# One pair of PSUM banks for two heads' scores in the attention mixers

## The chip, the cores and the metric

The kernel runs on one core of one Trainium2 chip. The metric is the device time of one execution in microseconds (us), as the median of repeated runs. The names of the engines in the rows are PE (matmul), PEld (weight load), DVE (VectorE), ACT (ScalarE), POOL (GpSimd) and SP (the engine that issues most transfers).

## The reference

Two layers of a diffusion backbone work on 256 context tokens and 256 latent tokens of width 1024. Each layer modulates its input with vectors computed from the conditioning, projects it, runs three groups of heads side by side (windowed attention A, a state space model B, differential attention C), projects their outputs and normalises. Layer 0 then runs a SwiGLU, layer 1 a mixture of 8 experts. Only the two attentions are touched by the change:

```python
# A: 6 query heads on 2 key heads of width 64, with a sink logit for each head
s = einsum(q, k) * 64 ** -0.5                  # latent: 512 keys, context: 256 keys
p = softmax(concat([s, sink]))                 # a band mask on the latent keys
y = einsum(p, v)

# C: 4 heads, each with two halves of width 32
s = einsum('bqhid,bkhid->bhiqk', q, k) * 32 ** -0.5
p = softmax(s)
a = p[:, :, 0] - lam * p[:, :, 1]
y = rmsnorm(einsum(a, v)) * (1 - lam_init)
```

## The kernel before, in words

Tokens lie in four tiles of 128 rows, two of context and two of latent tokens. Dense projections split each float operand in a high and a low half (`split`, L254 and L255) and make three matmuls of each (`mm3`, L268, L269 and L271). Weights come in through `load_w` (L246 to L249): a ring of four `raw` buffers, filled by transfers that SP issues in program order, so a buffer that is not given back holds up every later weight.

The function `mixers` of a layer starts several generators (dense projections, the three head groups, the output projection `op`, and `ada_group`, which computes modulation vectors for later from 64 tiny matmuls (L311) per group on weights `w_ada`) and `weave` takes their pieces in turn, by costs that each piece yields and by the weights in `PLAN`. A scheduler then fixes one order of instructions on each engine. Each engine runs its own list in that order and waits where an operand or a buffer is not there yet.

PSUM has eight banks of 128x512 floats. One pool shares them by tags: `S` three banks, `tp` two, `mm` two and `y` one. In the mixers `S` holds scores, `ada`, the token projections of the stage ahead (`TOKT`), the decayed products `p` (`T4`), `Sc` (`T5`) and `GT` (`T6`) of group B, and one of the two `xbc` projections.

An attention step is made of two heads. In `attn_A` (L865) a step is two key heads, whose score matmuls (L876) use 64 of the 128 rows of PE each; in `attn_C` (L901) it is the two halves of a head, with 32 rows each (L914). Each head has a bank of its own. `softmax` (L844) takes a maximum (L847), scales it (L849 or L851), and lets ACT write the exponentials `P` with their sum (L853). Group C then scales one half on ACT (L921), joins both with one product on DVE (L922), transposes the result (L860, copied by L862) and multiplies by the values (L927). Group A subtracts the sink, scales both heads (L890), transposes both and multiplies (L896). There are 42 steps: 14 with 256 keys, all in layer 0 (6 of A and 8 of C), and 28 with 512 keys (6 of A and 8 of C in each layer).

Of the kernel before, what the change touches and what calls it, by code (L numbers as in the profile page):

```python
# [12 lines left out]
F = mybir.dt.float32  # L13
# [3 lines left out]
AF = mybir.ActivationFunctionType  # L17
OP = mybir.AluOpType
AX = mybir.AxisListType.X
PSUM = bass.MemoryType.PSUM  # L20
# [5 lines left out]
LAT = (2, 3)  # L26
CTX = (0, 1)
# [17 lines left out]
CAPS, SLOTS = (64, 128, 128, 128, 128, 128, 64, 64), (0, 1, 6, 2, 7, 3, 4, 5)  # L45
NBUF = {"S": 3, "tp": 2, "mm": 2, "y": 1}
FDN = ("tp", "tp", "y", "mm"), ("S", "S", "S", "mm")
TOKT, TRA, ADA = "S", "tp", "S"
T1, T2, T3, T4, T5, T6, T7, T8, T9 = "y", "tp", "mm", "S", "S", "S", "mm", "tp", "tp"
OPT = 'mm'  # L50
HTD = 1
TL0 = CTX, LAT
# [58 lines left out]
def kernel(ctx: ExitStack, tc: tile.TileContext, I, out: bass.AP):  # L111
    nc = tc.nc
    V, S, G, T, SP = nc.vector, nc.scalar, nc.gpsimd, nc.tensor, nc.sync
# [4 lines left out]
    ps = ctx.enter_context(tc.tile_pool(name="ps", bufs=1, space=PSUM))  # L118
# [11 lines left out]
        return slice((t % 2) * 128, (t % 2) * 128 + 128)  # L130


    def p_(tag, name):
        return ps.tile([128, 512], F, name=name, tag=tag, bufs=NBUF[tag])

    def p_mm(name="mm"):
        return p_("mm", name)
# [68 lines left out]
    identb, maskF, maskB, ltb, onesb = (cb[:, i * 128:(i + 1) * 128] for i in range(5))  # L206
# [3 lines left out]
    def x_src(li, t):  # L210
        if li:
            return xscr[t * 128:(t + 1) * 128]
        return (I["ctx"] if t in CTX else I["x"])[0, (t % 2) * 128:(t % 2 + 1) * 128]


    def rstd_of(v, n, scale=1.0):
# [46 lines left out]
    def mm3(o, terms, start=True, stop=True):  # L263
# [6 lines left out]
        for i, (ah, al, bh, bl, wa) in enumerate(terms):  # L270
# [11 lines left out]
                    None, op0=OP.mult)  # L282
# [218 lines left out]
    def mixers(L, full_ctx, fill, tail):  # L501
# [5 lines left out]
        mp = att_ctx.enter_context(tc.tile_pool(name=f"att{li}", bufs=1, side="right"))  # L507
# [29 lines left out]
        def xbc_piece(f0, f1):  # L537
# [15 lines left out]

            if f0 == 0 and L.ready:

                pms = [p_mm("xbc"), p_("S", "xbc")]
                for ks in L.ready(sp, mp):
                    for k in ks:
                        for f in range(2):
                            mm(f, pms[f], 0, (k,))  # L560
                for f in range(2):
                    evac(f, pms[f], 0)
                    yield 5.1
                return
# [44 lines left out]
        def qTA(t):  # L609
            return yrow(t, 0, 3)  # L610

        def qTC(t):
            return yrow(t, 6, 8)
# [30 lines left out]

        def ktag(t):

            return "S" if t in CTX and not full_ctx else TOKT

        def use_C0(t, pm, a):
            V.tensor_tensor(dt[:, t], pm[:, 0:12], L.dtb, op=OP.add)  # L650
# [190 lines left out]
        def keys(t):  # L841
            return 256 if t in CTX else 512

        def softmax(po, n, nsink, sscale, st_, i):  # L844

            mx, nm, l = (st_[:, j, i:i + 1] for j in range(3))
            V.tensor_reduce(mx, po[:, :n], axis=AX, op=OP.max)  # L847
            if nsink is None:
                V.tensor_scalar(nm, mx, -sscale, None, op0=OP.mult)  # L849
            else:  # L850
                V.scalar_tensor_tensor(nm, mx, -sscale, nsink, op0=OP.mult, op1=OP.min)  # L851
            P = mp.tile([128, 512], F, name="P", tag="P", bufs=6)
            S.activation(P[:, :n], po[:, :n], AF.Exp, scale=sscale, bias=nm, accum_out=l)  # L853
            return P

        def transp(src, n):

# [7 lines left out]
        def attn_A(t):  # L865
            n = keys(t)
            nb = n // 128
            for g in range(3):
                st_ = sm.tile([128, 5, 2], F, name="smx", tag="smx", bufs=6)
                l, r, e = st_[:, 2], st_[:, 3], st_[:, 4]  # L870
                Ps, pos = [], []
                for kv in range(2):
                    po = p_("S", "SA")
                    pos.append(po)
                    b0 = 64 * kv
                    T.matmul(po[:, :n], qTA(t)[b0:b0 + 64, g], kTA[b0:b0 + 64, :n], start=True, stop=t in CTX)  # L876
                    if t == 2:
                        T.matmul(po[:, 384:512], identb, maskB, start=False, stop=True)
                    elif t == 3:
                        T.matmul(po[:, 256:384], identb, maskF, start=False, stop=True)  # L880
                for kv in range(2):
                    Ps.append(softmax(pos[kv], n, L.nsink[:, g, kv:kv + 1], 0.125, st_, kv))
                yield 0.0017 * n
                V.tensor_tensor(e, st_[:, 1], L.nsink[:, g], op=OP.subtract)
                S.activation(e, e, AF.Exp)
# [15 lines left out]
        def attn_C(t):  # L901
# [4 lines left out]
            for h in range(4):  # L906
                st_ = sm.tile([128, 5, 2], F, name="smx", tag="smx", bufs=6)
                l, r = st_[:, 2], st_[:, 3]
                Ps, pos = [], []
                for i in range(2):  # L910
                    po = p_("S", "SC")
                    pos.append(po)
                    b0 = 32 * ((2 * h + i) % 4)
                    T.matmul(po[:, :n], qTC(t)[b0:b0 + 32, h // 2], kTC[b0:b0 + 32, h // 2, :n], start=True,  # L914
                             stop=True)
                for i in range(2):
                    Ps.append(softmax(pos[i], n, None, 32 ** -0.5, st_, i))
                yield 0.0017 * n
                V.reciprocal(r, l)
                V.tensor_tensor(r[:, 1:2], r[:, 1:2], L.nlam, op=OP.mult)  # L920
# [796 lines left out]
                    yield v  # L1717

    mixers(L0, True, [ada_group(L0, 1), ada_group(L0, 2)], tail0())
    for _ in ada_group(L1, 0):  # L1720
        pass
    with tc.tile_pool(name="ffn", bufs=1) as fp:
# [2 lines left out]
    post.close()  # L1725


    for _ in layer_consts2(L1):
        pass

# [25 lines left out]
    mixers(L1, False, [ada_group(L1, 1), ada_group(L1, 2)], tail1())  # L1756
    tail_ctx.close()
    right.close()
    with ExitStack() as e:

        late = e.enter_context(tc.tile_pool(name="late", bufs=1))
        pools = [e.enter_context(tc.tile_pool(name=f"mraw{i}", bufs=1)) for i in range(3)]
        slots = [pools[i] for i, n in zip((1, 2, 0), MRB) for _ in range(n)]
        moe(L1, L1.pp, late, slots)
    post.close()


_INS = ["x", "c", "ctx", "c_ctx", "w_ada", "b_ada", "w_in", "attn_sink", "conv_w", "conv_b", "dt_bias", "a_log",
# [20 lines left out]
```

## Time and profile before

| what | value |
|---|---|
| median of 3 runs | 1867.69 us (1859.02 to 1873.53) |
| profiled execution | 1867.13 us, its span 1865.3 us |
| mean granted clock of PE | 0.96 of full speed |
| PE busy | 1712.7 us, 92% of the span |
| DVE, ACT, POOL busy | 1146.8, 873.3 and 327.9 us |

The profiled execution is one of the kernel before; 1.8 us of its time lie outside the span. The layer-0 mixers with their attention lie between some 60 and 400 us, the layer-1 mixers between some 850 and 1086 us. Between them stands the SwiGLU, behind them the experts.

### The profile page before, as it was taken

To read this page: it belongs to the slowest core of one execution; us is meant where nothing else is said; L and a number is where in the kernel's file an instruction comes from. 1 tells how busy PE (TensorE), PEld (TensorE's weight loads), DVE (VectorE), ACT (ScalarE), POOL (GpSimd) and SP (SyncE) were. 2 spreads that over 40 slices of the span, in tenths; PEclk is the share of its full clock that TensorE was granted. 3 is DMA by queue.
4 is the path that set the end of the run, shared out by engine and by line. 5 is a ranking of instruction groups with operands and counts; after the bars stand their busy time and mean duration, and the time that the engine had idled before them with its cause. 6 is when DMAs were issued, how large, how long until landed. Compare 5 with 4: busy or idle time off the path is not lost.

```text
span 1865.3 us, 26243 instructions
## 1 busy us (share of the span) xinstructions
PE 1712.7 (92%) x9355; PEld 1262.9 (68%) x9355; DVE 1146.8 (61%) x2242; ACT 873.3 (47%) x1460; POOL 327.9 (18%) x254
## 2 busy tenths in 40 slices
PE   5889999788999999979989949999999999999995
PEld 2677667576888888857866723486458537888884
DVE  4773577768433333485777670487068408898987
ACT  3533546437322233345435721375157317777774
POOL 1221023354310222952232420000000000000000
PEclk8999999798999999998999969999999999999998
DMA  9237254158432332546672359999999999999991
GB/s 309 79 105 229 81 173 150 46 173 257 125 102 89 93 101 90 164 154 216 200 228 72 109 183 397 409 406 401 369 409 406 380 396 408 408 370 359 340 324 50
DMA packets 251002, 436.37 MB, mean 234 GB/s; under 512 B 15056, under 2 KB 166232, under 8 KB 250864
## 3 DMA queue, kind: packets, MB, share of 16 engines
q1 hardware_dynamic: 248944, 429.81, 65.1%
q0 software_dynamic: 1920, 4.81, 0.9%
q8 instruction: 76, 1.25, 0.3%
q14 instruction: 62, 0.51, 0.1%
HBM read 431.34 MB, written 3.23 MB: 233 GB/s over the span
## 4 chain that ended last, share of the span: by engine, by line
PE 75%; DMA 8%; DVE 8%; issue 3%; ACT 2%; POOL 1%; SPq 0%; DVEq 0%; ACTq 0%; POOLq 0%
PE mg L1365 6%; PE mu L1365 5%; PE mdn L1365 5%; PE gu L271 4%; PE gu L268 4%; PE gu L269 4%; DMA raw<-in_w_ada 4%; PE mg L1519 3%; PE mg L1354 3%; PE mu L1519 3%; PE mu L1354 3%; PE mdn L1354 3%; DMA mraw<-in_exp_w_down 2%; PE tok L268 2%; PE tok L271 2%
## 5 line engine op out<-in xcount | busy, mean ns | idle before, releaser
L1345 DVE TENSOR_TENSOR mwl<-mraw,mwh 128x1024 fp32r<-128x1024 f32 (+2 forms) x372 | 388.7, 1103 | 26.1 <-ACT mwh L1344 18.3
L1344 ACT ACTIVATE mwh<-mraw 128x1024 fp32r<-128x1024 f32 (+2 forms) x372 | 339.8, 965 | 84.0 <-DMA mraw<-in_exp_w_gu 45.6
L255 POOL TENSOR_TENSOR wlo<-raw,whi 128x1024 fp32r<-128x1024 f32 (+2 forms) x93 | 230.7, 2487 | 480.5 <-ACT whi L254 422.2
L254 ACT ACTIVATE whi<-raw 128x1024 fp32r<-128x1024 f32 (+2 forms) x168 | 168.3, 1004 | 239.1 <-PE dn L269 71.9
L255 DVE TENSOR_TENSOR wlo<-raw,whi 128x1024 fp32r<-128x1024 f32 (+2 forms) x75 | 88.3, 1178 | 144.2 <-ACT whi L254 142.4
L268 PE MATMUL gu<-HI,whi 128*128 128x512 f32 (+1 forms) x400 | 144.4, 369 | 2.3 <-ACT whi L254 2.3
L269 PE MATMUL gu<-LO,whi 128*128 128x512 f32 (+1 forms) x400 | 144.9, 369 | 0.0
L311 PE MATMUL ada<-raw,cT 128*32 128x256 f32 x768 | 74.8, 429 | 41.8 <-DMA raw<-in_w_ada 38.3
L268 PE MATMUL tok<-whi,HI 128*128 128x256 f32 (+2 forms) x400 | 108.0, 299 | 4.4 <-ACT xin L545 3.1
L269 PE MATMUL tok<-whi,LO 128*128 128x256 f32 (+2 forms) x400 | 105.5, 293 | 5.3 <-DVE LO L439 4.1
L271 PE MATMUL gu<-HI,wlo 128*128 128x512 f32 (+1 forms) x400 | 98.5, 367 | 0.0
L268 PEld LDWEIGHTS tok<-whi,HI 128*128 128x128 f32 x400 | 78.6, 197 | 13.5 <-issue 4.4
L268 PEld LDWEIGHTS gu<-HI,whi 128*128 128x128 f32 x400 | 75.9, 191 | 15.8 <-ACT whi L254 2.5
L269 PEld LDWEIGHTS gu<-LO,whi 128*128 128x128 f32 x400 | 76.2, 191 | 12.7
L269 PEld LDWEIGHTS tok<-whi,LO 128*128 128x128 f32 x400 | 78.5, 197 | 9.2 <-DVE LO L439 5.9
L271 PEld LDWEIGHTS gu<-HI,wlo 128*128 128x128 f32 x400 | 70.3, 188 | 12.9
L268 PE MATMUL dn<-whi,ah 128*128 128x512 f32 x176 | 70.2, 399 | 4.9 <-ACT whi L254 4.9
L1354 PE MATMUL mdn<-mwl,mah 128*128 128x512 f32 x220 | 72.8, 399 | 0.9 <-DVE mwl L1345 0.5
L1365 PE MATMUL mdn<-mwh,mah 128*128 128x512 f32 x220 | 73.5, 399 | 0.0
L1528 DVE TENSOR_TENSOR msl<-msl,mu 128x512 f32<-128x512 f32 (+1 forms) x9 | 5.8, 643 | 110.0 <-PE mu L1519 110.0
L271 PE MATMUL tok<-wlo,HI 128*128 128x256 f32 (+2 forms) x400 | 71.4, 296 | 1.9 <-DVE nw L222 1.9
L1365 PE MATMUL mdn<-mwh,mal 128*128 128x512 f32 x220 | 72.5, 394 | 0.0
(358 smaller groups left out, 3645.6 us busy)
## 6 DMA issues: line engine op xcount, KB each, us to landing
mraw<-in_exp_w_gu SPq DMA_DIRECT2D x128, 1024.0 KB, 12.4
mraw<-in_exp_w_down SPq DMA_DIRECT2D x87, 1024.0 KB, 14.5
mraw<-in_exp_w_gu SPq DMA_DIRECT2D x64, 768.0 KB, 11.4
raw<-in_w_ada SPq DMA_DIRECT2D x88, 512.0 KB, 5.4
raw<-in_ffn_w_gu SPq DMA_DIRECT2D x100, 256.0 KB, 3.3
raw<-in_w_in SPq DMA_DIRECT2D x38, 512.0 KB, 5.1
raw<-in_ffn_w_down SPq DMA_DIRECT2D x30, 512.0 KB, 3.5
E<-cscr POOLq DMA_DIRECT2D x12, 384.0 KB, 7.1
```

The lines of the kernel that those rows point to most:

```text
L254: S.activation(hi, raw, AF.Copy)
L255: (eng or V).tensor_tensor(lo, raw, hi.bitcast(F), op=OP.subtract)
L268: T.matmul(o, ah, bh, start=start and i == 0, stop=False)
L269: T.matmul(o, *((ah, bl) if wa else (al, bh)), start=False, stop=False)
L271: T.matmul(o, *((al, bh) if wa else (ah, bl)), start=False, stop=stop and i == n - 1)
L311: T.matmul(pa[32 * j:32 * j + 32, hs], cT[:, k], w[j], start=(k == 0), stop=(k == KC - 1), tile_position=(0, 32 * j), skip_group_check=True)
L1344: S.activation(wh, raw, AF.Copy)
L1345: V.tensor_tensor(wl, raw, wh.bitcast(F), op=OP.subtract)
L1354: T.matmul(pc[:, :w], xh, wl[:, c * 512:c * 512 + w], start=False, stop=stop)
L1365: T.matmul(pc[:, :w], x, wh[:, c * 512:c * 512 + w], start=start and x is xh, stop=False)
L1519: T.matmul(p[hs, :n], Xf[:, kk, hs], raws[h][:, k, c * n:(c + 1) * n], start=kk == 0, stop=kk == KC - 1, skip_group_check=True)
L1528: V.tensor_tensor(sl[:, cs_], sl[:, cs_], p[:, :n], op=OP.mult)
```

## The change: one pair tile, one maximum, fewer banks for the others

In the mixers, `S` shrinks to one bank and a new tile `S2` of two adjacent banks, one buffer, takes the scores of both heads of a step. Both score matmuls are written one behind the other, the masks behind both. One reduction takes both maxima, one operation scales both, and ACT still writes two exponentials. What shared `S` before moves: the token projections, `p` and `GT` to `tp`, `Sc` and the second `xbc` to `mm`. In the dense stages `S` keeps three banks.

```diff
-TOKT, TRA, ADA = "S", "tp", "S"
-T1, T2, T3, T4, T5, T6, T7, T8, T9 = "y", "tp", "mm", "S", "S", "S", "mm", "tp", "tp"
+TOKT, TRA, ADA = "tp", "tp", "S"
+T1, T2, T3, T4, T5, T6, T7, T8, T9 = "y", "tp", "mm", "tp", "mm", "tp", "mm", "tp", "tp"
...
+    def stage(name):
+        if banks:
+            banks[0].close()
+        banks[:] = [ExitStack()]
+        banks.append(banks[0].enter_context(tc.tile_pool(name=name, bufs=1, space=PSUM)))
+        NBUF["S"] = 1 if name.startswith("mix") else 3
+
     def p_(tag, name):
-        return ps.tile([128, 512], F, name=name, tag=tag, bufs=NBUF[tag])
+        return (banks[1] if tag == "S" else ps).tile([128, 512], F, name=name, tag=tag, bufs=NBUF[tag])
+
+    def p_pair(name):
+        return banks[1].tile([128, 2, 512], F, name=name, tag="S2", bufs=1)
...
-                pms = [p_mm("xbc"), p_("S", "xbc")]
+                pms = [p_mm("xbc") for _ in range(2)]
...
-            return "S" if t in CTX and not full_ctx else TOKT
+            return "mm" if t in CTX and not full_ctx else TOKT
...
-        def softmax(po, n, nsink, sscale, st_, i):
-
-            mx, nm, l = (st_[:, j, i:i + 1] for j in range(3))
-            V.tensor_reduce(mx, po[:, :n], axis=AX, op=OP.max)
+        def softmax(po, n, nsink, sscale, st_):
+
+            mx, nm, l = (st_[:, j] for j in range(3))
+            V.tensor_reduce(mx, po[:, :, :n], axis=AX, op=OP.max)
...
-            P = mp.tile([128, 512], F, name="P", tag="P", bufs=6)
-            S.activation(P[:, :n], po[:, :n], AF.Exp, scale=sscale, bias=nm, accum_out=l)
-            return P
+            Ps = []
+            for i in range(2):
+                P = mp.tile([128, 512], F, name="P", tag="P", bufs=6)
+                S.activation(P[:, :n], po[:, i, :n], AF.Exp, scale=sscale, bias=nm[:, i:i + 1], accum_out=l[:, i:i + 1])
+                Ps.append(P)
+            return Ps
...
-                Ps, pos = [], []
+
+                po = p_pair("SA")
                 for kv in range(2):
-                    po = p_("S", "SA")
-                    pos.append(po)
-                    b0 = 64 * kv
-                    T.matmul(po[:, :n], qTA(t)[b0:b0 + 64, g], kTA[b0:b0 + 64, :n], start=True, stop=t in CTX)
...
-                for kv in range(2):
-                    Ps.append(softmax(pos[kv], n, L.nsink[:, g, kv:kv + 1], 0.125, st_, kv))
+                    bs = slice(64 * kv, 64 * kv + 64)
+                    T.matmul(po[:, kv, :n], qTA(t)[bs, g], kTA[bs, :n], start=True, stop=t in CTX)
+                if t in LAT:
+                    mask, ms_ = ((maskB, slice(384, 512)), (maskF, slice(256, 384)))[t - 2]
+                    for kv in range(2):
+                        T.matmul(po[:, kv, ms_], identb, mask, start=False, stop=True)
+                Ps = softmax(po, n, L.nsink[:, g], 0.125, st_)
...
-                Ps, pos = [], []
+                po = p_pair("SC")
                 for i in range(2):
-                    po = p_("S", "SC")
-                    pos.append(po)
-                    b0 = 32 * ((2 * h + i) % 4)
-                    T.matmul(po[:, :n], qTC(t)[b0:b0 + 32, h // 2], kTC[b0:b0 + 32, h // 2, :n], start=True,
-                             stop=True)
-                for i in range(2):
-                    Ps.append(softmax(pos[i], n, None, 32 ** -0.5, st_, i))
+                    bs = slice(32 * ((2 * h + i) % 4), 32 * ((2 * h + i) % 4) + 32)
+                    T.matmul(po[:, i, :n], qTC(t)[bs, h // 2], kTC[bs, h // 2, :n], start=True, stop=True)
+                Ps = softmax(po, n, None, 32 ** -0.5, st_)
...
+    stage("mix0")
...
     mixers(L0, True, [ada_group(L0, 1), ada_group(L0, 2)], tail0())
+    stage("dense0")
...
+    stage("mix1")
...
     mixers(L1, False, [ada_group(L1, 1), ada_group(L1, 2)], tail1())
...
+    stage("dense1")
```

In the orders below, `x2` behind a row means that it stands twice in a row, and the line numbers are those of each kernel: scores are L876 and L914 before, L893 and L928 after. On PE in layer 0, at the latent steps of group A, the two heads' scores (SA) stand apart before:

```order
L876 MATMUL SA<-kTA,YT 128x512
L878 LDWEIGHTS cb
L878 MATMUL SA<-cb 128x128
L896 MATMUL yA<-PT,vA 64x128 x4
L860 MATMUL PT<-cf,P 128x128 x2
L876 MATMUL SA<-kTA,YT 128x512
L878 LDWEIGHTS cb
L878 MATMUL SA<-cb 128x128
```

At the same place after, with the `ada` matmuls of the modulation behind the transposes:

```order
L893 MATMUL SA<-kTA,YT 128x512 x2
L897 LDWEIGHTS cb
L897 MATMUL SA<-cb 128x128
L897 LDWEIGHTS cb
L897 MATMUL SA<-cb 128x128
L912 MATMUL yA<-PT,vA 64x128 x4
L878 MATMUL PT<-cf,P 128x128 x4
L326 MATMUL ada<-raw,cT 32x256 x8
```

The scores of a step now follow each other, and so do its masks and its four transposes. On PE at the end of the layer-1 mixers, where the output projection (op) stands among the steps of group C, before:

```order
L271 MATMUL op<-wlo,HI 128x256 x2
L914 MATMUL SC<-kTC,YT 128x512
L860 MATMUL PT<-cf,P 128x128
L927 MATMUL yC<-vC,PT 128x64 x4
L860 MATMUL PT<-cf,P 128x128 x3
L914 MATMUL SC<-kTC,YT 128x512 x2
L268 MATMUL op<-whi,HI 128x256
L269 MATMUL op<-whi,LO 128x256
```

The last four steps of group C in that stage after:

```order
L928 MATMUL SC<-kTC,YT 128x512 x2
L286 MATMUL op<-wlo,HI 128x256
L939 MATMUL yC<-vC,PT 128x64 x4
L878 MATMUL PT<-cf,P 128x128 x4
L939 MATMUL yC<-vC,PT 128x64 x4
L928 MATMUL SC<-kTC,YT 128x512 x2
L878 MATMUL PT<-cf,P 128x128 x4
L939 MATMUL yC<-vC,PT 128x64 x4
L928 MATMUL SC<-kTC,YT 128x512 x2
L878 MATMUL PT<-cf,P 128x128 x4
L939 MATMUL yC<-vC,PT 128x64 x4
L928 MATMUL SC<-kTC,YT 128x512 x2
```

The rest of the output projection now stands ahead of these steps. On DVE in layer 1 before, maxima of later heads (L847) stand ahead of the product of an earlier step (L922):

```order
L847 TENSOR_REDUCE smx<-SC 128x1
L849 TENSOR_SCALAR smx<-smx 128x1
L847 TENSOR_REDUCE smx<-SC 128x1
L922 SCALAR_TENSOR_TENSOR P<-P,smx 128x512
L849 TENSOR_SCALAR smx<-smx 128x1
L919 RECIPROCAL smx<-smx 128x2
L847 TENSOR_REDUCE smx<-SC 128x1
L920 TENSOR_TENSOR smx<-smx,lcst 128x1
```

The same steps on DVE after, maximum (L862) and product (L934):

```order
L862 TENSOR_REDUCE smx<-SC 128x2
L864 TENSOR_SCALAR smx<-smx 128x2
L931 RECIPROCAL smx<-smx 128x2
L932 TENSOR_TENSOR smx<-smx,lcst 128x1
L934 SCALAR_TENSOR_TENSOR P<-P,smx 128x512
L942 TENSOR_TENSOR yC<-yC,lcst 128x64
L862 TENSOR_REDUCE smx<-SC 128x2
L864 TENSOR_SCALAR smx<-smx 128x2
```

Each step is now finished on DVE, up to its product, ahead of the maximum of the next.

## Rows read from the trace of the kernel before

**Rows 1.** Profile page, part 4: share of the ending chain by engine

```profile
PE 75%; DMA 8%; DVE 8%; issue 3%; ACT 2%; POOL 1%; SPq 0%; DVEq 0%; ACTq 0%; POOLq 0%
```

**Rows 2.** Windows: stretch, length; busy PE, PEld, DVE, ACT, POOL; granted clock, DMA share, GB/s

```profile
183.00:250.00 67.00, 67.00 (x493) 44.50 (x495) 43.91 (x141) 35.22 (x108) 4.75 (x2) 1.00 0.33 101
...
340.00:360.00 20.00, 14.25 (x58) 9.12 (x56) 13.28 (x51) 8.31 (x27) 9.30 (x7) 0.74 0.15 41
...
360.00:380.00 20.00, 14.57 (x60) 10.46 (x60) 12.29 (x53) 11.19 (x32) 2.05 (x3) 0.66 0.00 0
...
987.00:1054.00 67.00, 66.05 (x415) 44.36 (x415) 50.42 (x155) 43.73 (x107) 15.15 (x12) 0.97 0.30 93
...
1054.00:1072.00 18.00, 17.86 (x146) 16.73 (x145) 7.56 (x20) 9.91 (x25) 9.99 (x8) 1.00 0.15 54
```

**Rows 3.** Timeline of PE at scores: start, length (us), engine, line, operation, count

```profile
183.70 0.70 PE L876 MATMUL SA<-kTA,YT 64*128 64x256 f32 x4
...
197.12 0.70 PE L876 MATMUL SA<-kTA,YT 64*128 64x256 f32 x2
...
209.07 1.12 PE L876 MATMUL SA<-kTA,YT 64*128 64x512 f32 x2
210.13 0.44 PE L860 MATMUL PT<-cf,P 128*128 128x128 f32 x2
...
363.10 2.00 PE L914 MATMUL SC<-kTC,YT 32*128 32x512 f32 x2
...
1024.74 1.13 PE L914 MATMUL SC<-kTC,YT 32*128 32x512 f32 x4
...
1027.41 1.89 PE L914 MATMUL SC<-kTC,YT 32*128 32x512 f32 x4
...
1030.84 1.55 PE L914 MATMUL SC<-kTC,YT 32*128 32x512 f32 x4
...
1037.09 1.59 PE L914 MATMUL SC<-kTC,YT 32*128 32x512 f32 x4
```

**Rows 4.** Tile view of SA, the maxima: count, min/median/max (ns) of one

```profile
L847 DVE TENSOR_REDUCE smx<-SA x36: 414/684/692, 184.4 to 1017.3; 128x1 f32<-128x512 f32 x24, 128x1 f32<-128x256 f32 x12
```

**Rows 5.** Timeline of PE, DVE and ACT, parts of C steps in layer 1

```profile
1049.65 1.13 PE L914 MATMUL SC<-kTC,YT 32*128 32x512 f32 x4
...
1050.81 0.69 DVE L847 TENSOR_REDUCE smx<-SC 128x1 f32<-128x512 f32 x1 [0.73 <-PE SC L914]
...
1052.88 0.67 ACT L853 ACTIVATE P<-SC,smx 128x512 f32<-128x512 f32 x1
...
1054.95 0.75 DVE L922 SCALAR_TENSOR_TENSOR P<-P,smx 128x512 f32<-128x512 f32 x1 [0.92 <-ACT P L921]
...
1056.08 0.68 DVE L847 TENSOR_REDUCE smx<-SC 128x1 f32<-128x512 f32 x1
...
1057.09 0.68 ACT L853 ACTIVATE P<-SC,smx 128x512 f32<-128x512 f32 x1
```

**Rows 6.** Timeline of PE at the end of the layer-1 mixers

```profile
1063.02 0.28 PE L268 MATMUL op<-whi,HI 128*128 128x256 f32 x1
1063.14 0.28 PE L269 MATMUL op<-whi,LO 128*128 128x256 f32 x1
...
1071.28 1.10 PE L927 MATMUL yC<-vC,PT 128*128 128x64 f32 x8
```

**Rows 7.** Windows as in Rows 2, ahead of the layer-0 attention

```profile
120.00:130.00 10.00, 10.00 (x89) 7.71 (x87) 7.71 (x26) 3.70 (x11) 3.39 (x6) 1.00 0.02 4
130.00:140.00 10.00, 7.89 (x66) 6.38 (x58) 3.67 (x13) 1.31 (x3) 3.71 (x3) 1.00 0.95 276
```

**Rows 8.** Timeline of PE, the ada matmuls; in brackets a wait and its releaser

```profile
128.73 1.91 PE L311 MATMUL ada<-raw,cT 128*32 128x256 f32 x26
...
141.78 1.08 PE L311 MATMUL ada<-raw,cT 128*32 128x256 f32 x8 [3.37 <-DMA raw<-in_w_ada]
```

**Rows 9.** Profile page, part 5: the high halves, with mean ns

```profile
L254 ACT ACTIVATE whi<-raw 128x1024 fp32r<-128x1024 f32 (+2 forms) x168 | 168.3, 1004 | 239.1 <-PE dn L269 71.9
```

More of the change, by code (lines that the diff above doesn't have):

```diff
@@ L130, in tcol @@
         return slice((t % 2) * 128, (t % 2) * 128 + 128)
+    banks = []
+    def stage(name):
[4 more added lines that the diff above has]
+        NBUF["S"] = 1 if name.startswith("mix") else 3
     def p_(tag, name):
-        return ps.tile([128, 512], F, name=name, tag=tag, bufs=NBUF[tag])
+        return (banks[1] if tag == "S" else ps).tile([128, 512], F, name=name, tag=tag, bufs=NBUF[tag])
+    def p_pair(name):
+        return banks[1].tile([128, 2, 512], F, name=name, tag="S2", bufs=1)
     def p_mm(name="mm"):
@@ L870, in attn_A @@
                 l, r, e = st_[:, 2], st_[:, 3], st_[:, 4]
-                Ps, pos = [], []
+                po = p_pair("SA")
                 for kv in range(2):
-                    po = p_("S", "SA")
-                    pos.append(po)
-                    b0 = 64 * kv
-                    T.matmul(po[:, :n], qTA(t)[b0:b0 + 64, g], kTA[b0:b0 + 64, :n], start=True, stop=t in CTX)
[L877 to L880, printed above, removed]
-                for kv in range(2):
-                    Ps.append(softmax(pos[kv], n, L.nsink[:, g, kv:kv + 1], 0.125, st_, kv))
+                    bs = slice(64 * kv, 64 * kv + 64)
[5 more added lines that the diff above has]
+                Ps = softmax(po, n, L.nsink[:, g], 0.125, st_)
                 yield 0.0017 * n
@@ L1765 @@
     post.close()
+    banks[0].close()
 _INS = ["x", "c", "ctx", "c_ctx", "w_ada", "b_ada", "w_in", "attn_sink", "conv_w", "conv_b", "dt_bias", "a_log",
```

## Prediction

> **What bounds the kernel now.** I first read the share of the chain that ended last [rows 1]: three quarters of it is PE. Work taken off PE can therefore shorten the kernel, while DVE and ACT count only where PE waits for them. Then I read the windows of the stages that the change reaches [rows 2]. In layer 0, where attention begins (183 to 250), PE is busy 67.00 of 67.00 us at full granted clock; there PE is the bound. At the end of that stage (340 to 380) it is busy 28.82 of 40 at a granted clock of 0.74 and 0.66: there it waits for the softmax, some 11 us of it. In layer 1 it is busy 66.05 of 67.00 (987 to 1054) and 17.86 of 18.00 behind that. The SwiGLU loop and the experts keep their order in the changed kernel, so everything has to come from the two mixers. A measurement of this kernel can tell about 1% (18.7 us) from no change.
>
> **What pairing takes off PE.** A score uses 64 or 32 of PE's 128 rows, on row groups of its own for each head. The timeline [rows 3] shows both forms already. Context: the two matmuls of one head take 0.70 us (197.12), and the four of two heads that stand side by side also 0.70 (183.70). The second head is free. Latent: one head takes 1.12 and the next instruction starts 1.06 later (209.07 to 210.13); two heads side by side take 1.13 (1024.74). So a step newly put together saves 0.64 (0.70 less the same overlap of 0.06) or 1.06. In the order of before 11 of the 42 steps stand together already (2 in A and 4 in C of layer 0, 5 in C of layer 1); after, all do. That gives: A, context, 4 x 0.64 = 2.6; A, latent, 12 x 1.06 = 12.7, half in each layer; C in layer 0, (5 x 0.64) + (7 x 1.06) = 10.6; C in layer 1, 3 x 1.06 = 3.2, and in steps that already stand together but whose second head waits for a bank (1.89, 1.55 and 1.59 instead of 1.13) 0.76 + 0.42 + 0.46 = 1.6. Sum: **30.7 us**, 19.5 in layer 0 and 11.1 in layer 1. Of layer 0 I take 17.3, since by the new order 2.2 of other work moves in between the first score and the last. Fewer changes between part and all of the rows I cost at 0, with bounds of 0 and -3 (31 steps by a tenth at most: a transpose starts right at the end of a score, 210.13 behind 209.07 [rows 3]).
>
> **What the single pair tile adds.** Two heads used to have three banks in turn, and maxima of later heads stood on DVE ahead of the product of an earlier step. Now there is one pair tile, and DVE's order finishes each step up to its product before the next maximum. That makes a loop. Its length for a latent C step: the joint maximum, not seen before; 512 elements take 0.684 and 256 take 0.414 [rows 4], so 0.27 for 256 and 0.684 + 2 x 0.27 = 1.22 for 1024 (bounds: 0.68, the single one, and 1.37, twice that); from a maximum's end to an exponential 0.33 (1056.76 to 1057.09); one exponential to the next 0.67; from the second one's start to the end of the product 2.82 (1052.88 to 1055.70) [rows 5]. Sum **5.0 us**. The path through the tile itself is shorter (second exponential's end, next score, its maximum 1.16 behind it: 1.83 instead of 2.82), so DVE's order binds. A latent A step comes to 4.6, since its loop ends with two scalings instead of reciprocal, ACT scaling and product, and a context step to 3.6.
>
> Against it stands PE's work between two scores in the new order, from the durations of before: transposes, value products, dense matmuls, ada. A bare latent C step is 1.06 for scores, 4 x 0.22 for transposes and half of 1.10 for the values [rows 3, 6], some 2.5. Where other work fills the gap to over 5 us, the loop costs nothing. In layer 0 the sums are below it at 11 of the steps: by 0.5, 1.1 and 2.1 in latent A, and by 1.5, 0.6, 0.4, 1.6, 3.9, 1.5, 2.7 and 3.5 in C, together **19.4 us**. Its cover elsewhere is the dense and state-space work of the stage, with all other segments between 4.4 and 23.3 us. About half of these steps lie at the end of the stage, where PE waits anyway [rows 2], so I take half: 9.7 (bounds 0 and 19.4). Layer 0: -17.3 + 9.7 = **-7.6**.
>
> In layer 1 the new order has 69.7 us of PE work from the first score to the last. The loop lengthens six of the 13 segments, by 0.6 + 0.5 + 2.1 (the third with the gating of group B on DVE) in A and 1.6 + 2.5 + 2.5 in C, where the last four steps have no output projection between them any more: 9.8. Behind the last score comes the end of a chain, 1.16 + 5.0 + transposes, copy and values, 8.4 together. That is 87.9. Before, the first score to the last value product took 85.2 (987.1 to 1072.38 [rows 6]), less 1.1 for nine dense matmuls, each 0.12 [rows 6], that now stand ahead of the first score: 84.1. So layer 1: **+3.8** (bounds -11.1, with all of the pairing kept, and +8, with a lower clock in the idle end as in [rows 2]).
>
> A rule of the Trainium skill speaks against this change: the page "TensorEngine Tiling (Array Packing)", section "PSUM Bottleneck", says that tiling speeds up the matmuls but not the emptying of PSUM, which may then become the bottleneck. The rows agree in kind, with 5.0 us of max, exponentials and product against 2.5 of PE. By that rule alone the time would be that of the second rival.
>
> **What the banks move.** In layer 0 the transfers of weights stop for a while: the DMA share is 0.02 in 120 to 130 and 0.95 in the 10 us behind it [rows 7], because ada tiles that landed earlier sit in the raw ring until PE comes to their 26 matmuls at 128.73; then PE waits 3.37 for the next ones [rows 8]. In the new order the first eight ada matmuls stand some 25 us earlier, so buffers come back earlier. I take -2; bounds -7 (both waits behind the stop gone) and +3 (one more wait like that, since PE's list is in order and a matmul that waits for weights holds all behind it). The `tp` banks, which now also serve `p`, `GT` and the token projections besides the transposes, I cost at 0: PE is busy without a gap in 183 to 250 with the old sharing, and I cannot read the new one; the step that has to wait there waits for one copy on ACT, so the bounds are those of a rival below. Masks only change places, and the second scaling and the second maximum cost DVE nothing that PE waits for beyond the loop.
>
> **Sum.** -7.6 + 3.8 - 2 = -5.8. The profiled execution (1867.13) and the median (1867.69) are the same to 0.6, so the forecast is 1867.7 - 5.8 = **1862 us**, and 1854 to 1871 with the smaller unknowns.
>
> **Rivals.** *The pairing is kept whole.* If the loop's waits fall where PE waited before, or ACT and DVE run ahead of their place in my sums, all 30.7 and the 2 of ada remain: 1835. For it speaks that PE has 11 us of idle time at the end of layer 0, and that the joint maximum saves DVE time; against it that layer 1 has almost no idle time now, so waits in its last steps would be new. Half way to it would be 1849.
>
> *The loop takes all back.* With PE busy nearly throughout, every microsecond of shortfall is new: -17.3 + 19.4 + 3.8 = +5.9, or 1874. For it: 67.00 of 67.00 busy in the first part of the attention [rows 2], where no older wait can hide it. Against: 340 to 380.
>
> *Slower: other ACT work queues within the loop.* The loop passes through ACT three times. High halves of weights, 1.00 us each [rows 9], stand in ACT's list between exponentials and the scaling. Before, another step's scores were waiting in banks, so such a detour cost PE little. With one in each of some 16 latent steps that have no slack, it is 16 x 1.0 on top of the second rival: 1890. It decides when the maxima of successive unfilled C steps stand over 6 us apart instead of 5.0. Against it: in the last layer-1 steps few weights are left to be split.
>
> **How the numbers follow.** Forecast 0.50; pairing kept 0.23; loop takes all 0.14; ACT in the loop 0.13. Likeliest is the forecast, 1862. The range leaves out most of the slower rival (0.10) and the low end of the first (0.08): 1840 to 1885. It covers the bounds of ada and of the loop in layer 0. Faster by over 1% (below 1849): most of the first rival and the edge of the forecast, 0.25. Slower by over 1% (above 1886): 0.13. Within 1%: 0.62.
>
> **What would show it.** In the profile after: scores as x4 at 1.1 to 1.2 us throughout; a maximum of 1024 elements at about 1.22; successive maxima of the last four C steps of layer 1 some 5 us apart, with PE idle about half of that and a lower granted clock; layer-1 scores to last value product at 87 to 89; layer-0 first to last score some 172 instead of 179.4 (183.7 to 363.1 [rows 3]). I would be wrong if the `tp` banks hold up the transposes, if the loop is under 4 us, or if the earlier ada matmuls make PE wait for weights.

## The result

The changed kernel is slower: 1925.72 us median (1918.92 to 1928.39, 4 runs) against 1870.51 for the kernel before, measured beside it. The ratio is 1.0301, with a 95% interval of 1.0248 to 1.0354. Forecast were 1862 and a range of 1840 to 1885. The profiled execution took 1925.32 us, 58.2 more than that of before.

The first line below is part 4 of the page of the changed kernel, the share of the ending chain by engine; the second is the engines' busy time from part 1.

```profile
PE 69%; DVE 11%; DMA 9%; ACT 3%; issue 3%; POOL 0%; SPq 0%; DVEq 0%; ACTq 0%; POOLq 0%
...
PE 1727.1 (90%) x9355; PEld 1280.1 (67%) x9355; DVE 1168.0 (61%) x2158; ACT 876.8 (46%) x1460; POOL 319.3 (17%) x254
```

Against [rows 1], PE's share of the chain fell from 75% to 69%, and DVE's rose from 8% to 11%. PE is busy 14.4 us longer, although the pairing should have taken 30.7 off it, and idle 43.8 us longer (1923.5 - 1727.1 = 196.4 instead of 1865.3 - 1712.7 = 152.6).

By stage, from the starts of the score matmuls and of the SwiGLU's and experts' matmuls in the tile views of both traces:

| stretch (us) | before | after | difference |
|---|---|---|---|
| layer 0: start to first score | 183.7 | 194.3 | +10.6 |
| first to last score | 180.4 | 205.4 | +25.0 |
| last score to first SwiGLU matmul | 74.2 | 66.4 | -7.8 |
| layer 1: last gate or up matmul (`gu`) of the SwiGLU to first score | 233.9 | 248.8 | +14.9 |
| first to last score | 73.0 | 95.4 | +22.4 |
| last score to first expert matmul | 65.4 | 58.6 | -6.8 |

The loss lies in both mixers: 47.4 us between the scores and 25.5 ahead of them, where the pairing does nothing yet; 14.6 are given back behind them. The windows of the changed kernel, columns as in [rows 2]:

```profile
120.00:140.00 20.00, 18.28 (x141) 12.25 (x139) 8.20 (x32) 4.80 (x15) 3.10 (x5) 0.83 0.64 200
140.00:160.00 20.00, 13.83 (x91) 10.43 (x92) 12.31 (x33) 5.00 (x8) 4.08 (x3) 0.80 0.56 165
...
360.00:380.00 20.00, 10.79 (x52) 7.83 (x49) 15.30 (x48) 9.25 (x25) 8.88 (x7) 0.68 0.28 73
380.00:400.00 20.00, 15.37 (x64) 9.40 (x62) 13.64 (x53) 9.71 (x31) 2.55 (x2) 0.67 0.00 1
...
1100.00:1120.00 20.00, 17.02 (x81) 11.43 (x81) 9.74 (x25) 12.54 (x33) 3.78 (x4) 0.70 0.00 1
1120.00:1140.00 20.00, 13.70 (x46) 9.11 (x42) 11.11 (x41) 5.42 (x16) 3.45 (x4) 0.62 0.00 0
```

The stretch without weight transfers that [rows 7] showed at 120 to 130 is gone (a DMA share of 0.64). But PE now runs 120 to 160 at a granted clock of 0.83 and 0.80, where the same 40 us of before had 1.00 and 0.91. Busy time says little there: in 120 to 140 PE is busy 18.28 us with 141 matmuls, where it was busy 17.89 us with 148 before.

The timeline of PE in the changed kernel, at scores, with waits in brackets:

```profile
373.43 1.22 PE L928 MATMUL SC<-kTC,YT 32*128 32x256 f32 x4 [8.09 <-ACT P L870]
...
1024.90 1.13 PE L893 MATMUL SA<-kTA,YT 64*128 64x512 f32 x4
...
1046.60 1.13 PE L893 MATMUL SA<-kTA,YT 64*128 64x512 f32 x4 [0.91 <-ACT P L870]
```

Pairs stand together. With 512 keys they take 1.13 us where the granted clock is 1.00 (the last two lines), as in [rows 3]; the pair of 256 keys in the first line takes 1.22 instead of 0.70, in a stretch with a clock of 0.68. What this takes off PE stands in the groups of score matmuls (count, busy us, mean ns; idle time before them), before:

```profile
L914 PE MATMUL SC<-kTC,YT 32*128 32x512 f32 x64 | 32.2, 654 | 0.4 <-ACT P L853 0.4
L876 PE MATMUL SA<-kTA,YT 64*128 64x512 f32 x48 | 26.9, 641 | 0.0
L914 PE MATMUL SC<-kTC,YT 32*128 32x256 f32 x32 | 11.3, 457 | 0.3 <-ACT P L853 0.3
L876 PE MATMUL SA<-kTA,YT 64*128 64x256 f32 x24 | 7.0, 428 | 0.0
```

and after:

```profile
L928 PE MATMUL SC<-kTC,YT 32*128 32x512 f32 x64 | 23.6, 821 | 6.8 <-ACT P L870 6.6 <-ACT kTC L650 0.3
L893 PE MATMUL SA<-kTA,YT 64*128 64x512 f32 x48 | 14.5, 682 | 2.9 <-ACT P L870 2.9
L928 PE MATMUL SC<-kTC,YT 32*128 32x256 f32 x32 | 6.6, 497 | 13.3 <-ACT P L870 13.3
L893 PE MATMUL SA<-kTA,YT 64*128 64x256 f32 x24 | 4.2, 428 | 0.0
```

Scores keep PE busy for 48.9 us instead of 77.4, 28.5 less. So the pairing does what it should, and everything else on PE got 42.9 us longer. The scores now wait for the exponentials of the step ahead, 17.4 us in all at C steps of layer 0:

```profile
PE SC L928 <- ACT P L870: 17.4, 6, 8.1
```

One turn of the loop among the last C steps of layer 1, from the timeline of PE, DVE and ACT:

```profile
1115.68 1.23 DVE L862 TENSOR_REDUCE smx<-SC 128x2 f32<-128x1024 f32 x1 [0.61 <-PE SC L928]
1116.72 0.60 ACT L880 ACTIVATE PT<-PT 128x512 f32<-128x512 f32 x1 [2.37 <-PE PT L878]
1116.94 0.17 DVE L864 TENSOR_SCALAR smx<-smx 128x2 f32<-128x2 f32 x1
1117.21 0.68 ACT L870 ACTIVATE P<-SC,smx 128x512 f32<-128x512 f32 x1
1117.37 1.97 PE L939 MATMUL yC<-vC,PT 128*128 128x64 f32 x8 [0.69 <-ACT PT L880]
...
1117.87 0.69 ACT L870 ACTIVATE P<-SC,smx 128x512 f32<-128x512 f32 x1
...
1119.27 2.08 PE L928 MATMUL SC<-kTC,YT 32*128 32x512 f32 x4
...
1119.89 0.75 DVE L934 SCALAR_TENSOR_TENSOR P<-P,smx 128x512 f32<-128x512 f32 x1 [0.85 <-ACT P L933]
1120.56 0.22 DVE L942 TENSOR_TENSOR yC<-yC,lcst 128x64 f32<-128x64 f32 x1
1121.28 1.11 PE L878 MATMUL PT<-cf,P 128*128 128x128 f32 x4
1121.39 1.22 DVE L862 TENSOR_REDUCE smx<-SC 128x2 f32<-128x1024 f32 x1 [0.61 <-PE SC L928]
```

The joint maximum takes 1.22 to 1.23, as forecast. The turn takes 5.71 us (1115.68 to 1121.39). DVE is done with its product at 1120.64 and would be ready; what ends its last wait is PE. The pair tile is free at 1118.56, but the next scores stand behind the value matmuls, which take 1.97 here against 1.10 for the same eight in [rows 6], and take 2.08 themselves instead of 1.13. The granted clock is 0.50 from 1113.56 to 1119.27, the lower of its two levels (1.2 GHz); it was 1.00 in 1102.5 to 1107.6, where PE was busy 3.81 of 5.10 us. At the lower level the matmuls of the turn, and with them the loop, take longer.

### The profile page after: what moved, and what is told of

It is laid out like the page before. It is cut to its first block, busy times and chain, and to the rows that moved or that the text cites. A ratio compares the mean times of both kernels' runs of the same rounds, so it can differ in the third digit from the quotient of the medians.

```text
span 1923.5 us, 26170 instructions
## 1 busy us (share of the span) xinstructions
PE 1727.1 (90%) x9355; PEld 1280.1 (67%) x9355; DVE 1168.0 (61%) x2158; ACT 876.8 (46%) x1460; POOL 319.3 (17%) x254
## 4 chain that ended last, share of the span: by engine, by line
PE 69%; DVE 11%; DMA 9%; ACT 3%; issue 3%; POOL 0%; SPq 0%; DVEq 0%; ACTq 0%; POOLq 0%
PE mg L1377 5%; PE mu L1377 5%; PE mdn L1377 5%; PE gu L286 4%; PE gu L283 4%; PE gu L284 4%; DMA raw<-in_w_ada 4%; PE mg L1531 4%; PE mu L1531 3%; DMA mraw<-in_exp_w_down 3%; PE mg L1366 3%; PE mu L1366 3%; PE mdn L1366 3%; PE tok L283 2%; PE tok L284 2%
## 5 line engine op out<-in xcount | busy, mean ns | idle before, releaser
L270 POOL TENSOR_TENSOR wlo<-raw,whi 128x1024 fp32r<-128x1024 f32 (+2 forms) x93 | 222.6, 2399 | 461.6 <-ACT whi L269 425.7
L326 PE MATMUL ada<-raw,cT 128*32 128x256 f32 x768 | 77.4, 440 | 45.6 <-DMA raw<-in_w_ada 43.9
L283 PEld LDWEIGHTS gu<-HI,whi 128*128 128x128 f32 x400 | 75.7, 191 | 15.9 <-ACT whi L269 2.7
L1377 PE MATMUL mg<-mwh,Xh 128*128 128x512 f32 x240 | 72.5, 383 | 0.0
L1377 PE MATMUL mu<-mwh,Xh 128*128 128x512 f32 x240 | 71.2, 378 | 1.0 <-ACT mwh L1356 1.0
## 6 DMA issues: line engine op xcount, KB each, us to landing
mraw<-in_exp_w_down SPq DMA_DIRECT2D x87, 1024.0 KB, 14.6
mraw<-in_exp_w_gu SPq DMA_DIRECT2D x64, 768.0 KB, 10.6
```

The costliest lines, as they stand in the source:

```text
L270: (eng or V).tensor_tensor(lo, raw, hi.bitcast(F), op=OP.subtract)
L283: T.matmul(o, ah, bh, start=start and i == 0, stop=False)
L326: T.matmul(pa[32 * j:32 * j + 32, hs], cT[:, k], w[j], start=(k == 0), stop=(k == KC - 1), tile_position=(0, 32 * j), skip_group_check=True)
L1377: T.matmul(pc[:, :w], x, wh[:, c * 512:c * 512 + w], start=start and x is xh, stop=False)
```

## The experiments

The theory on record was that the loop of the one pair tile costs what the pairing saves. Rival: the other PSUM users, which the prediction had costed at nothing. Each ratio is to the kernel before, run beside it on the same chip. Every edit also lets the scheduler fix new orders on all engines, so a run changes more than its edit; no run kept the order.

**The parts one by one.** First run: the kernel before with only the moved users.

```diff
-TOKT, TRA, ADA = "S", "tp", "S"
-T1, T2, T3, T4, T5, T6, T7, T8, T9 = "y", "tp", "mm", "S", "S", "S", "mm", "tp", "tp"
+TOKT, TRA, ADA = "tp", "tp", "S"
+T1, T2, T3, T4, T5, T6, T7, T8, T9 = "y", "tp", "mm", "tp", "mm", "tp", "mm", "tp", "tp"
```

(with the second xbc and the context keys of layer 1 on mm too). 

> Scores as before (a bank and a maximum for each head, three S banks), only the other users of PSUM on the tags of the change (token projections, p and GT on tp, Sc and the second xbc on mm). Theory 1 (the serial loop of the one pair tile costs the time): within 12 us of the kernel before, 1860 to 1880. Rival (the moved PSUM users cost it, by waits ahead of and between the scores): 1900 to 1925, most of the 55 us. If half of it is each's: 1890 to 1900.

Measured: 1923.43, ratio 1.028 (1.0217 to 1.0343), against 1.0301 for the whole change. My theory fell here: the moved users alone cost 53 us.

Second run: the changed kernel with a maximum for each head.

```diff
-            V.tensor_reduce(mx, po[:, :, :n], axis=AX, op=OP.max)
...
             for i in range(2):
+                c = slice(i, i + 1)
+                V.tensor_reduce(mx[:, c], po[:, i, :n], axis=AX, op=OP.max)
```

(a scaling for each head too)

> The changed kernel with the one pair tile kept, but a maximum and a scaling for each head as before. If the joint maximum is what lengthens the loop: 15 to 30 us below the changed kernel, since the first exponential then starts 0.5 us earlier in 42 steps and the order gets free; if the joint release of the tile is what counts: within 10 us of the changed kernel, 1916 to 1936.

Measured: 1933.56, ratio 1.0318 (1.0257 to 1.0379). The joint maximum is no loss as such. Third run: two single banks instead of the pair tile, with a maximum for each head.

```diff
-        return banks[1].tile([128, 2, 512], F, name=name, tag="S2", bufs=1)
+        return [banks[1].tile([128, 512], F, name=name, tag="S2", bufs=2) for _ in range(2)]
```

> The changed kernel with two banks of their own for the two heads of a step instead of the pair tile, and a maximum for each head: a bank comes free as soon as its own exponential is done. Theory 1: the wait for the pair is relaxed, 25 to 45 us below the changed kernel, 1880 to 1900. Rival (moved users): within 12 us of the changed kernel, 1914 to 1938.

Measured: 1934.85, ratio 1.0326 (1.0268 to 1.0384): giving the banks back one by one gains nothing. Fourth run: the maximum taken out of the loop.

```diff
-            V.tensor_reduce(mx, po[:, :, :n], axis=AX, op=OP.max)
-            if nsink is None:
-                V.tensor_scalar(nm, mx, -sscale, None, op0=OP.mult)
-            else:
-                V.scalar_tensor_tensor(nm, mx, -sscale, nsink, op0=OP.mult, op1=OP.min)
+            V.memset(nm, 0.0)
```

> The changed kernel without the maximum: the exponentials take a shift of zero instead of the row's maximum, so that the reduction of 1.22 us and its scaling leave the loop (this leaves out the guard against overflow; the quotient is the same in exact arithmetic). Theory 1: 28 latent steps lose 1.5 us and 14 context steps 1.0 of loop, over 56 us in all, of which half or more is time: 1880 to 1900. Rival: 0 to 15 us below the changed kernel, 1910 to 1926.

Measured: 1892.58, ratio 1.0109 (1.0054 to 1.0165). So the maximum in the loop has a price too, 33 us. By stage, as in the table above, each against the kernel before:

| stretch (us) | changed | moved users alone | changed, no maximum |
|---|---|---|---|
| layer 0: start to first score | +10.6 | +5.0 | +5.0 |
| first to last score | +25.0 | +18.8 | +5.6 |
| last score to first SwiGLU matmul | -7.8 | +0.4 | -2.4 |
| layer 1: last `gu` to first score | +14.9 | +25.7 | +19.5 |
| first to last score | +22.4 | +10.3 | +6.4 |
| last score to first expert matmul | -6.8 | -4.0 | -9.1 |

The moved users lose most between the scores of layer 0 and ahead of those of layer 1. Without the maximum 19.4 and 16.0 us come back between the scores, where the loop is.

**Is it the loop of the pair?** The same edit in the kernel before, and in the kernel with the moved users alone:

> The kernel before without the maximum (a shift of zero in the exponentials, which leaves out the guard against overflow). The changed kernel lost 33 us by the same edit. If those 33 are the loop of the single pair tile: here 0 to 12 us below the kernel before, 1858 to 1871. If they are DVE work that any version waits for: 20 to 33 below, 1838 to 1850.

> The run with all other PSUM users moved and scores as before, now without the maximum (a shift of zero, no guard against overflow). The changed kernel without it came to 1892.6. If pairing does save some 31 us on PE and its loop gives them back through the maximum: 1915 to 1926 here, as the kernel before loses nothing by the same edit. If the 33 us are the moved users' and not the pair's: 1888 to 1900.

Measured: 1873.12, ratio 1.0035 (1.0003 to 1.0067), and 1933.19, ratio 1.0345 (1.0319 to 1.0371). Without the pair tile the maximum costs nothing that ends up in the time; with it, 33 us. And without the maximum, the pair is worth 1892.6 - 1933.2 = -40.6 on the moved users (-30.8 against the run with its maxima). The second of these runs came out 7 us above its range, and 10 above the same kernel with its maxima, so that much can come from a new order alone. The page of three kernels, part 1: moved users alone, moved users without the maximum, and the changed kernel without the maximum.

```profile
PE 1742.1 (91%) x9355; PEld 1283.0 (67%) x9355; DVE 1168.9 (61%) x2242; ACT 878.6 (46%) x1460; POOL 323.3 (17%) x254
```

```profile
PE 1767.4 (91%) x9355; PEld 1295.6 (67%) x9355; DVE 1116.3 (58%) x2158; ACT 881.4 (45%) x1460; POOL 320.2 (17%) x254
```

```profile
PE 1711.2 (90%) x9355; PEld 1273.3 (67%) x9355; DVE 1120.2 (59%) x2116; ACT 878.2 (46%) x1460; POOL 322.6 (17%) x254
```

The paired kernel without its maximum has 30.9 us less of PE busy time than the first (1742.1 - 1711.2) and the same idle time (1891.2 - 1711.2 = 180.0, and 1921.7 - 1742.1 = 179.6). Against the second, which also lacks the maximum, it has 56.2 less, so such differences hold the clock as well as the pairing. Busy time times the mean granted clock of the span, a rough estimate of the work, is 1641, 1638 and 1609 (clocks 0.942, 0.927 and 0.940), 1644 before (0.960) and 1611 in the changed kernel (0.933): the pair takes some 30 off in each comparison. The changed kernel, with its maximum, has 196.4 idle and 1727.1 busy: between these two runs the maximum costs 15.9 us of busy time on as many matmuls and 16.4 of idle time.

**Which moved user?** From the kernel before, one group each: B's three (p, GT to tp, Sc to mm), the token projections, the second xbc, Sc alone.

```diff
-T1, T2, T3, T4, T5, T6, T7, T8, T9 = "y", "tp", "mm", "S", "S", "S", "mm", "tp", "tp"
+T1, T2, T3, T4, T5, T6, T7, T8, T9 = "y", "tp", "mm", "S", "mm", "S", "mm", "tp", "tp"
```

(the edit for Sc alone)

> The kernel before with group B's three PSUM users alone on the tags of the change (p and GT on tp, Sc on mm). The run with all tags moved cost 53 us. Theory 2 (group B's chain of copies and products through the shared tp and mm banks is what costs it): 1905 to 1925. Rival (token projections or xbc): 1862 to 1882.

> The kernel before with the transposed token projections alone moved (from S to tp, and to mm for the context keys of layer 1). Theory 2: 1862 to 1882. Rival (the projections cost it): 1895 to 1925.

> The kernel before with the second of the two xbc projections alone moved from S to mm. It has both mm banks for the length of one projection at the start of a stage, so the dense matmuls behind it wait once in layer 0. Theory 2: 1862 to 1882. Rival (the xbc projection costs it): 1885 to 1925.

> The kernel before with group B's Sc alone moved from S to mm, where the dense projections accumulate; p and GT stay on S. If the cost of group B is Sc's, whose two matmuls wait for products on DVE and so keep a dense bank waiting: 1895 to 1920, near the run with all three moved. If it is p's and GT's on tp: 1862 to 1882.

| moved alone | median | ratio (95% interval) |
|---|---|---|
| p, GT and Sc | 1898.47 | 1.0153 (1.0107 to 1.0199) |
| token projections | 1888.85 | 1.0118 (1.0063 to 1.0174) |
| second xbc | 1871.69 | 1.0012 (0.9988 to 1.0037) |
| Sc | 1894.40 | 1.0115 (1.0064 to 1.0167) |

Group B costs 1.5%, most of it Sc's; the token projections 1.2% (17 us); xbc nothing. Neither B alone nor the projections alone reach what theory or rival wanted of them: both count. Sc's 1894.4 lies just below its range. The reverse, Sc back on S with all others moved:

> The run with all other PSUM users moved and scores as before (1923), with Sc alone back on S. Sc moved alone cost 21 us. If the costs add: 1898 to 1906. If the other users fill the gap: 1915 or more.

Measured: 1915.27, ratio 1.0246 (1.0219 to 1.0273). That is 8 us below the run with all moved, not 21: the costs do not simply add.

**Is it the dense banks that Sc takes, or any move?** Sc alone on y and on tp:

> The kernel before with Sc alone moved from S to y (one bank, used by group B's own diagonal product and the attention outputs) instead of mm. If the 21 us of Sc on mm come from the dense products that lose a bank: 1864 to 1878. If any move of Sc away from the three S banks costs it: 1885 or more.

> The kernel before with Sc alone moved from S to tp, the two banks of the transposes. If the dense banks are the point: 1864 to 1880, some more than on y at most. If any move costs: 1885 or more.

Measured: 1896.23, ratio 1.0131 (1.01 to 1.0161) on y, and 1870.65, ratio 1.0016 (0.999 to 1.0043) on tp. Neither expectation fits both: the dense banks are not the whole of it, since y costs as much, and not every move costs, since tp is free. What sets the costly places of Sc apart shows in the windows of the dense token matmuls alone (count in brackets, then granted clock, DMA share, GB/s), the same 40 us in before, Sc on tp, Sc on mm, Sc on y and the changed kernel:

```profile
120.00:140.00 20.00, 7.31 (x56) 1.00 0.48 140
140.00:160.00 20.00, 11.88 (x83) 0.91 0.74 220
```

```profile
120.00:140.00 20.00, 3.32 (x24) 0.97 0.72 208
140.00:160.00 20.00, 15.32 (x96) 0.86 0.65 195
```

```profile
120.00:140.00 20.00, 1.91 (x14) 0.82 0.64 203
140.00:160.00 20.00, 9.79 (x72) 0.84 0.77 226
```

```profile
120.00:140.00 20.00, 3.32 (x24) 0.83 0.54 169
140.00:160.00 20.00, 7.47 (x44) 0.83 0.78 234
```

```profile
120.00:140.00 20.00, 2.72 (x19) 0.83 0.64 200
140.00:160.00 20.00, 8.52 (x56) 0.80 0.56 165
```

Here group B's chain of layer 0 begins: small matmuls that wait for copies on ACT and products on DVE. The dense matmuls are what PE can do in between. Before there are 139 of them in these 40 us, with Sc on tp 120; with Sc on mm 86, on y 68, in the changed kernel 75. Where they are missing, the granted clock is 0.80 to 0.84, and the median of the eight Sc matmuls between 60 and 180 is 0.71 (mm), 0.59 (y) and 0.85 us (changed) instead of 0.49 (before and on tp). This sorts Sc's places only: with the token projections alone moved there are 124 dense matmuls at 1.00 and 0.91, and the 17 us are lost elsewhere, between the scores (+7.8 in layer 0, +13.2 in layer 1). The timeline of PE at Sc in layer 1, before and after:

```profile
937.92 1.56 PE L767 MATMUL Sc<-xw,Bt 128*128 128x384 f32 x4
...
945.91 1.56 PE L767 MATMUL Sc<-xw,Bt 128*128 128x384 f32 x4
```

```profile
971.57 2.93 PE L782 MATMUL Sc<-xw,Bt 128*128 128x384 f32 x4 [2.31 <-ACT Bt L766]
...
981.48 2.85 PE L782 MATMUL Sc<-xw,Bt 128*128 128x384 f32 x4 [2.20 <-DVE xw L772]
```

Two of these are 8.0 us apart before and 9.9 after, and PE now comes to them before their operands are there. The granted clock at the first is 1.00 before (937.9 to 939.4) and 0.50 after (971.5 to 974.4).

**Can the pairing be kept without the moves?** In the changed kernel: Sc in the two halves of the pair tile, which is idle while group B leads; then the token projections on it too; Sc on y; and all moved users back on S, which has one bank there.

```diff
-                pm = p_(T5, "Sc")
+                pm = pp[:, g]
```

(`pp` is one pair tile for both g)

> The changed kernel with both Sc products of a tile in the two halves of the pair tile instead of a dense bank (mm) each. Theory 2 (Sc's place on the dense banks costs some 21 us, the retag as a whole 53, and the pairing itself about 0): 1898 to 1912. If the pair tile, held while Sc waits for DVE, costs as much as the dense bank did: 1918 to 1935.

> As the run with Sc on the pair tile, and the transposed token projections on one half of the pair tile too, so that tp is free of them as before. Theory 2 (17 us for these on tp): 1880 to 1898. If the single pair buffer is now the narrow place: above the run with Sc alone there, 1910 or more.

> The changed kernel with Sc on y instead of mm. Sc on the pair tile came to 1907. If only the dense banks matter: 1900 to 1912 again. If y, which every step of attention needs for its output, is a narrower place: 1918 or more.

> The changed kernel with all the other PSUM users back on S, which has one bank here and is shared with ada: the pairing with the old sharing, as far as eight banks allow it. Theory 2 says that moved users wait for banks; here six users share one bank that ada holds for long stretches, so it is slower than the changed kernel or near it, 1920 to 1960. If the tags as such (tp and mm) were the harm, and not the number of banks: 1870 to 1895.

| changed kernel with | median | ratio (95% interval) |
|---|---|---|
| Sc on the pair tile | 1907.07 | 1.0207 (1.0186 to 1.0228) |
| and the projections too | 1903.17 | 1.0184 (1.0164 to 1.0204) |
| Sc on y | 1922.71 | 1.0282 (1.024 to 1.0324) |
| all back on S | 1916.44 | 1.0266 (1.023 to 1.0302) |

Sc on the pair tile gives back 19 us, as expected; the projections 4, not 17, between the two ranges; y, as before, gives nothing. With all back on S the time is 9 below the changed kernel and just under the lower end of its range: the tags tp and mm as such are not the harm, one bank of S for all is nearly as bad. The best of them and the maximum taken out:

> The changed kernel with Sc and the token projections on the pair tile (1903) and without the maximum (a shift of zero, no guard against overflow). If the two costs are independent: 1903 - 33 = 1870, at 1862 to 1880. If the pair tile's new users have taken over the waiting: 1885 or more.

Measured: 1867.79, ratio 0.9994 (0.9973 to 1.0015). That is 35 us below the run with its maximum. Both costs together are as large as the whole loss, but this kernel has no guard in its exponentials and is no faster than the kernel before, although its pairs save PE time too. Part 1 of its page:

```profile
PE 1703.3 (91%) x9355; PEld 1264.6 (68%) x9355; DVE 1113.8 (60%) x2116; ACT 876.7 (47%) x1460; POOL 324.1 (17%) x254
```

PE is only 9.4 us less busy than before (1712.7) and 10.4 us longer idle (163.0 against 152.6), so some 30 us more are lost, and no run shows to what: `p`, `GT`, the second `xbc`, the loop without its maximum or the order. No version beat the kernel before.

## Why the prediction was wrong

**The failed step is "what the banks move".** It costed the `tp` banks at 0 and did not price Sc on `mm` at all; its -2 stood for the weight transfers. Measured were +53 for this part by itself, Sc and the token projections above all. The reason given was that PE is busy without a gap in 183 to 250 with the old sharing. But by the tile views of before, the moved users (token projections, `p`, Sc, `GT`) run from 104 to 280 and again from 841 to 1019, and that they do no harm with three banks of `S` says nothing about two of `tp` or `mm`. The loss came elsewhere than in that window, where PE with the moved users alone is busy too (67.00 of 67.00 us, at a clock of 1.00): behind it in layer 0, and ahead of the scores in layer 1.

**The ada part was mis-sized too.** It was -2, with +3 as its upper bound. Over the whole execution PE's waits for these weights (us, times, longest) grew by 5.6, before and after:

```profile
PE ada L311 <- DMA raw<-in_w_ada: 38.3, 21, 9.0
```

```profile
PE ada L326 <- DMA raw<-in_w_ada: 43.9, 27, 10.0
```

In layer 0 they fell from 16.0 to 13.6 between 50 and 440, but rose by 3.3 behind that; in layer 1 they rose from 7.5 to 11.6. With the moved users alone they are 45.2, so this is a part of what the moved users cost, and one of the signs of being wrong that the prediction named.

**The pairing was sized about right.** 30.7 us were forecast, and the score matmuls take 28.5 less in the changed kernel itself, some of them at the lower clock.

**The loop was seen, and somewhat too small.** Its terms were 9.7 in layer 0 and 14.9 in layer 1 (3.8 with the 11.1 of the pairing taken off), 24.6 in all. Taking out the maximum alone gives 33. The turn was forecast as 5.0 with DVE's order binding. It took 6.02, 6.01 and 5.71 in the unfilled steps (maxima at 1103.65, 1109.67, 1115.68 and 1121.39), with PE binding in the last: I worked it out at full clock, while there the clock is at its lower level. The forecast of 172 from first to last score of layer 0 met 205.4, but the moved users alone make it 199.2, so this does not show how much of the loop hid under older waits. On top of the moved users the pair costs 1925.7 - 1923.4 = +2.3, where -17.3 - 11.1 + 24.6 = -3.8 was forecast. So pair and loop came out near the forecast, in part by luck, since the turn was too short; the miss is the moved users.

**The start of layer 1** was read as 987.1. The tile view of before has its first score at 981.9, with both heads of a step one behind the other up to 984.2, which were overlooked. By the same working the term would have been about -1 instead of +3.8, or +1.5 if the 2.9 us of other work up to 987.1 also moves ahead of the first score. It does not matter for the outcome.

**The rivals.** The slower one had the right sign and a wrong place: ACT work in the loop. The unfilled steps stand at its mark of 6 us, but between 1103.7 and 1121.4 ACT splits no weight. In the filled steps splits do stand on ACT, but the longest turn there (maxima at 1088.82 and 1097.01, 8.2 us apart) holds something else, the joint scaling of two columns on DVE beside a split on POOL. Before, one column beside such a split, and after, two:

```profile
1049.77 2.37 POOL L255 TENSOR_TENSOR wlo<-raw,whi 128x1024 fp32r<-128x1024 f32 x1
...
1049.93 0.14 DVE L849 TENSOR_SCALAR smx<-smx 128x1 f32<-128x1 f32 x1
```

```profile
1089.45 2.36 POOL L270 TENSOR_TENSOR wlo<-raw,whi 128x1024 fp32r<-128x1024 f32 x1
...
1090.07 1.76 DVE L864 TENSOR_SCALAR smx<-smx 128x2 f32<-128x2 f32 x1
```

The scaling, 0.17 us elsewhere, takes 1.76 and ends within 0.03 of POOL's instruction. All five scalings of this form that took over 0.5 us end so, 5.7 us together; in the second run, with a maximum and a scaling for each head, all 48 scalings of one column in group C took 0.15 at most. It is not what the change lost, since that run is no faster. The 16 us on top were neither needed nor shown. That moved PSUM users could be a rival of their own with a price was not considered.

By the Trainium skill, "TensorEngine Tiling (Array Packing)", section "PSUM Bottleneck", tiling speeds up the matmuls but not the emptying of PSUM, which may then become the bottleneck. These runs agree in kind for this pair: taking the maximum, which reads the scores from PSUM, out of the loop gives back 33 us, and none without the pair.

What stays open: why Sc costs as much on y as on mm and nothing on tp, and why its 21 us become 8 when the others have moved. The trace shows dense matmuls displaced and the clock down where Sc costs; which bank wait made the scheduler displace them was not separated, nor was the new order from the banks. Not run were a third bank for the scores of the changed kernel and the new pool of each stage by itself.

## What to carry to other kernels

A change that needs banks has two prices, its own and that of whoever gives them up. Price each displaced user in every stretch where it runs, and try the displacement alone first. A loop through one buffer is to be priced at the clock that PE gets when it idles in that loop. Taking out one operation in versions with and without the buffer tells whether the loop or the operation costs.

## What was not expected of the hardware

PE's busy share hides its clock. In 120 to 140, PE is busy 17.89 of 20 us before and 18.28 after, at granted clocks of 1.00 and 0.83; four Sc matmuls take 1.56 at one level (a granted clock of 1.00, 2.4 GHz) and 2.93 at the other (0.50, 1.2 GHz). With the same 9355 matmuls, the kernel with only the moved users is 29.4 us busier (1742.1 against 1712.7) and 27.0 us idler (179.6 against 152.6). Busy time times the mean clock of the span is 1641 and 1644, so by this estimate the added busy time is the lower clock's, about as much again as the added idle time.

A scaling of 128x2 numbers on DVE took 0.17 us by itself and up to 1.78 beside an instruction on POOL, until that one ended; with a scaling of 128x1 for each head, all 48 in group C took 0.14 or 0.15, beside POOL too.
